# Squares on ScalarE, row-scale chain emitted first, casts and diagonals on GpSimd: one edit in a two-layer mLSTM / sparse-attention kernel

## The chip, the cores and the metric

The kernel runs on 1 core of one Trainium2 chip. The metric is device time in microseconds of one execution; lower is better. A profiled execution has a time of its own and a span, which reaches from its first to its last instruction.

## The reference

A trunk of two layers over 256 tokens of width 1024, in float32. Each layer adds to x a mixer of the RMS-normalised x. Layer 0 is an mLSTM block with four heads of width 512, layer 1 a sparse-attention block with 16 heads. A final RMS norm follows.

```python
def rmsnorm(x, g):
    y = x * lax.rsqrt(jnp.mean(x * x, axis=-1, keepdims=True) + 1e-6)
    return y * g

def mlstm_mixer(h, w_in, conv_w, conv_b, w_q, w_k, w_v, w_if, b_if, ln_w, skip, w_out):
    x_in, z = jnp.split(h @ w_in, 2, axis=-1)                 # 1024 -> 2 x 2048
    conv = sum(x_pad[:, tap:tap + S] * conv_w[tap] for tap in range(4))
    x_conv = jax.nn.silu(conv + conv_b)
    q, k, v = headwise(x_conv, w_q), headwise(x_conv, w_k), headwise(x_in, w_v)   # 4x4 blocks
    gates = jnp.concatenate([q, k, v], -1) @ w_if + b_if
    hh = mlstm_chunkwise(q, k, v, gates ...)
    ...
    return ((hn + skip * x_conv) * jax.nn.silu(z)) @ w_out

x = x + mlstm_mixer(rmsnorm(x, ml_norm), ...)
x = x + nsa_mixer(rmsnorm(x, nsa_norm), ...)
return rmsnorm(x, final_norm)
```

## The kernel before

Every large product is made from three matmuls with operands split in a high and a low part (hi x hi, hi x lo, lo x hi). A weight unit (1 MB) is loaded as two halves (tile wr, SP's queue, L273); ScalarE rounds each half to its high part (wh, L274), and the low part (wl) is the difference, made by VectorE (L280) or, for the units in BY_DMA, by ScalarE and an accumulating DMA from GpSimd's queue (L277, L278). next_unit keeps LOOK = 2 units loaded ahead; ahead(n) writes the loads of the first n units.

The first layer's input comes transposed, as four chunks (xch0). ScalarE makes the high part of x times the gain (hh, L342) and VectorE the low part (hl, L343). The row scale 1/sqrt(mean x^2 + eps) isn't applied to x but to the products: the squares of x (sq1, L354) are summed over chunks (L356, L385), over partitions by a small matmul with ones (L388), get mean and epsilon (L323) and the power -1/2 on GpSimd (L325); two diagonal matrices (dg, L377) and a matmul with ones (L378) spread the result over all partitions, and it is copied to rb1 (L389), with half of it in rb1h (L390). norm1 writes this chain; the first evacuation of the first projection calls it.

The projection of the mLSTM block (project_channels, L411) runs unit by unit into PSUM; evac_x multiplies by rb1 (L438). The loads of cst (masks and block mask), wif (gate weights) and x each wait for rb1 by way of a one-element copy (L441, L445, L448), since they are written behind it in SP's queue. Per head there follow: block-diagonal weights on GpSimd (blockdiag, L398, which needs cst), gate weights on VectorE (L463, L464, which need wif), a convolution of four taps (L476, L480 on ScalarE, L482 on GpSimd, L487 on VectorE), and small projections (L497, L504, L511). In the second layer rstd_of and token_rows are used again for r2.

Instructions are put in each engine's queue when the program is built: a planner walks the written order with a model of the times and gives each engine the earliest written instruction that is ready in the model. So the order in a queue isn't the written one, and on the chip each queue runs strictly in its order.

Of the kernel before, what the change touches and what calls it, by code (L numbers as in the profile page):

```python
# [11 lines left out]
AF = mybir.ActivationFunctionType  # L12
OP = mybir.AluOpType
# [3 lines left out]
P = 128  # L17
S = 256
D = 1024
KT = D // P  # L20
# [37 lines left out]
ZF = 1  # L58
ZT = 3
WARM = 9  # L60
N0 = 2
CA_ = (1, 2, 3)
CB_ = (0,)
CH = 1
SQA = (2, 3)
SQP = (1, 2)
XT = 'zt'
NOT_POOL = (0, 1, 2, 11)
BOTH = (15, 16, 17)
# [133 lines left out]
def trunk(ctx, tc, a, out, dbg=None):  # L203
    nc = tc.nc
# [8 lines left out]
    def tile_of(pl, shape, dt=F32, tag=None, bufs=1, name=None):  # L213
        uid[0] += 1
        n = f"{name or tag}_{uid[0]}"
        return pl.tile(shape, dt, tag=tag or n, bufs=bufs, name=n)

    def T(*x, **k):
        return tile_of(pool[0], *x, **k)

    def TS(*x, **k):
        return tile_of(sb, *x, **k)

    def PS(shape=(P, 512), tag="ps", name="ps"):
        uid[0] += 1
        return pp.tile(list(shape), F32, tag=tag, bufs=PSB[tag], name=f"{name}_{uid[0]}")

    f32 = lambda t: t.bitcast(F32)
    V, A, GP, PE = nc.vector, nc.scalar, nc.gpsimd, nc.tensor
# [9 lines left out]
    xch0 = [T([P, 4, S], tag="zt", bufs=ZT, name="xch0") for _ in range(2)]  # L239
# [9 lines left out]
    pka = T([P, NC_A], name="pka")  # L249
    pkb = TS([P, NC_B], name="pkb")  # L250

    C = lambda n: cst[:, _C[n][0]:_C[n][1]]
    CA = lambda n: pka[:, _A[n][0]:_A[n][1]]
    CB = lambda n: pkb[:, _B[n][0]:_B[n][1]]
    ident = pk0[:, 0:P]
    gain1 = pk0[:, P:]
# [38 lines left out]
    def ahead(n):  # L295
        while len(loaded) < min(n, len(plan)):
            loaded.append(load_unit(*plan[len(loaded)]))
# [11 lines left out]
    first = TS([P, 1], name="first")  # L309
# [9 lines left out]
    def rstd_of(ms, n, name):  # L319

        k = ms.shape[1]
        me = T([P, k], name=name + "me")
        V.tensor_scalar(me, ms, 1.0 / n, 1e-6, op0=OP.mult, op1=OP.add)  # L323
        r = T([P, k], name=name)
        GP.tensor_tensor(r, me, mhalf[:, 0:k], op=OP.pow)  # L325
        return r

    ahead(N0)
    nc.sync.dma_start(pka, a["pka"])

    def transposed(kts, src, gain):

# [7 lines left out]
    def scaled(kts, at, gain):  # L340
        for kt in kts:
            A.activation(hh[:, kt, :], at(kt), AF.Copy, scale=gain[:, kt:kt + 1])  # L342
            V.scalar_tensor_tensor(hl[:, kt, :], at(kt), gain[:, kt:kt + 1], f32(hh[:, kt, :]),  # L343
                                   op0=OP.mult, op1=OP.subtract)

    def new_h():
        return [TS([P, KT, S], F32R, tag="hT", bufs=2) for _ in range(2)]

    hh, hl = new_h()
    sq1 = T([P, 4, S], tag="zt", bufs=ZT, name="sq1")  # L350
    for q in range(4):
        x_ = xch0[q // 2][:, 2 * (q % 2):2 * (q % 2) + 2, :]
        o_ = sq1[:, 2 * min(q, 1):2 * min(q, 1) + 2, :]
        (A.activation(o_, x_, AF.Square) if q in SQA else GP.tensor_tensor(o_, x_, x_, op=OP.mult))  # L354
        if q:
            (GP if q in SQP else V).tensor_tensor(sq1[:, 0:2, :], sq1[:, 0:2, :], o_, op=OP.add)  # L356
    scaled(range(KT), lambda kt: xch0[kt // 4][:, kt % 4, :], gain1)

    def squares(ss, n, tb):
        junk = T([P, 512], tag="sq", bufs=1, name="junk")  # L360
# [2 lines left out]
    def token_scale(ss, name):  # L363

        ms = T([P, 2], name=name + "ms")
        V.tensor_reduce(ms, ss, axis=AX.X, op=OP.add)
        return rstd_of(ms, D, name)
# [4 lines left out]
    def token_rows(r, bank, **place):  # L372

        dg = T([P, 2, P], name="dg", **place)
        ps = PS((P, S), tag=bank)
        for tb in range(2):
            V.tensor_scalar(dg[:, tb, :], ident, r[:, tb:tb + 1], None, op0=OP.mult)  # L377
            PE.matmul(ps[:, tb * P:(tb + 1) * P], onesq, dg[:, tb, :], start=True, stop=True)  # L378
        return ps, dg

    rb1 = T([P, S], name="rb1")
    rb1h = T([P, S], name="rb1h")

    def norm1():
        V.tensor_tensor(sq1[:, 0, :], sq1[:, 0, :], sq1[:, 1, :], op=OP.add)  # L385
        ps = PS((P, 2, 2))
        for tb in range(2):
            PE.matmul(ps[:, tb, :], sq1[:, 0, tb * P:(tb + 1) * P], onesq[:, 0:2], start=True, stop=True)  # L388
        V.tensor_copy(rb1, token_rows(rstd_of(ps[:, :, 0], D, "r1"), "ps")[0])  # L389
        V.tensor_scalar(rb1h, rb1, 0.5, None, op0=OP.mult)  # L390

    spread = lambda r: r[:, None, :].to_broadcast([P, 2, S])

    bm = C("bm")[:, None, :, None].to_broadcast([P, 4, 32, 4])
# [36 lines left out]
    for h in range(NH):  # L431
        xin = T([P, 4, S + 3], tag="xin", bufs=2)
        GP.memset(xin[:, :, 0:3], 0.0)
        for u in range(2):
            def evac_x(ps, x_=xin[:, 2 * u:2 * u + 2, 3:], first=(h, u) == (0, 0)):
                if first:
                    norm1()
                V.tensor_tensor(x_, ps, spread(rb1), op=OP.mult)  # L438
            project_channels(a["wi1"], 2 * h + u, evac_x, ("px", "px", "acc1")[(2 * h + u) % 3])
            if (h, u) == (0, 0):  # L440
                V.tensor_copy(cst[:, 0:1], rb1[:, 0:1])  # L441
                nc.sync.dma_start(cst, a["cst"][:, 0:n_res])
                wifs = [T([P, 16, n // 128, 8], tag="zt", bufs=ZT, name="wif") for n in (1024, 512)]
                for t, o_, n in zip(wifs, (0, 1024), (1024, 512)):
                    V.tensor_copy(t[:, 0, 0, 0:1], rb1[:, 0:1])  # L445
                    nc.sync.dma_start(t.rearrange("p a b c -> p (a b c)"), a["wif"][:, o_:o_ + n])
                for i in range(2):
                    V.tensor_copy(xt[i][:, 0, 0:1], rb1[:, 0:1])  # L448
                    nc.sync.dma_start(xt[i], a["x"][:, i * 512:(i + 1) * 512].rearrange("(t p) c -> p t c", p=P))
# [41 lines left out]
        q = T([P, 4, SG], tag="r4", bufs=8, name="q")  # L491
        gate_weights(q[:, :, S:SG], wqk, wifs[0], 2)
        for c2 in range(2):
            ps = PS((P, 2, S))
# [6 lines left out]
        for tb in range(2):  # L501
            ps = PS((P, 3, PG), tag="pt")
# [6 lines left out]
        ps = PS()  # L509
# [9 lines left out]
        scs.append(sc)  # L519

    ident_r = TS([P, P], F32R, name="ident_r")
    V.tensor_copy(ident_r, ident)
    maskt_r = T([P, 2, P], F32R, name="maskt_r")
    V.tensor_copy(maskt_r, C("maskt")[:, None, :].to_broadcast([P, 2, P]))
    causal = C("mask2")

    vsps = []
# [52 lines left out]
    ps = PS((P, 2, 64))  # L580
# [10 lines left out]
    for h in range(NH):  # L591
# [25 lines left out]
        r = sm("r")  # L617
# [28 lines left out]
    for h in range(NH):  # L646
# [8 lines left out]
        for c2 in range(2):  # L655
            ps = PS((P, 2, S))
# [4 lines left out]
            for c in range(2):  # L661
                k = 2 * c2 + c
                V.scalar_tensor_tensor(y[:, k, :], ps[:, c, :], lnw[:, 4 * h + k:4 * h + k + 1], y[:, k, :],
                                       op0=OP.mult, op1=OP.add)
# [79 lines left out]
    transposed(range(4, 8), x_cols, gain2)  # L744
    r2 = token_scale(ss2, "r2")
    ps, dg = token_rows(r2, "acc0", tag="p0", bufs=PB)
    rb = T([P, S], name="rb")
    V.tensor_copy(rb, ps)
# [395 lines left out]
```

## Time and profile before

| | us |
|---|---|
| three runs | 380.86, 381.38, 384.1 |
| median | 381.38 |
| profiled execution, time | 378.87 |
| profiled execution, span | 377.1 |
| mean granted TensorE clock | 0.984 |

The profiled execution lies 2.5 us under the median of the runs. In the profile, PE is TensorE's matmuls, DVE is VectorE, ACT is ScalarE, POOL is GpSimd, SP issues most loads. "Idle" stands in brackets at the end of a row of the timeline, with what ended it; a row that merges several instructions says so by x and a number.

### The profile page before, as it was taken

Reading aid. Unit: us, or ns where it says so; the run is one execution under the profiler, and the core shown is the slowest. Engines: PE = TensorE matmul, PEld = TensorE weight load, DVE = VectorE, ACT = ScalarE, POOL = GpSimd, SP = SyncE. Lnnn points to the kernel's source line nnn. Section 1 sums busy time; section 2 is a strip of 40 time slices with the busy share of each in tenths; the row PEclk is TensorE's granted clock in tenths of the full one; section 3 lists DMA queues with packets and bytes.
Section 4 is the critical chain, followed back from the end, with each engine's and each line's share of the span. In section 5 each row is a group of like instructions: output and inputs, shape, how many; then the busy total and the mean of one; then the engine's idle time right before and its main releaser. Section 6 shows DMA issues by size and latency. Waiting matters only on the chain.

```text
span 377.1 us, 6621 instructions
## 1 busy us (share of the span) xinstructions
PE 350.6 (93%) x2399; PEld 313.8 (83%) x2399; DVE 255.7 (68%) x535; ACT 241.5 (64%) x438; POOL 134.7 (36%) x165
## 2 busy tenths in 40 slices
PE   6998799979999979999999799999879999999991
PEld 6998799869998968988887699999869996777771
DVE  5976999756476548983243736687979789684515
ACT  6674669738468649765653744372579789996304
POOL 5226377433301124610100303283430283857003
PEclk9999899999999999999999999999989999999997
DMA  7889758765646978999998897546577865020003
GB/s 260 280 269 315 209 129 217 188 152 125 167 157 159 197 210 217 228 233 296 239 262 239 266 343 216 173 104 155 154 195 209 246 237 158 2 56 2 2 0 112
DMA packets 21633, 69.57 MB, mean 185 GB/s; under 512 B 2528, under 2 KB 2912, under 8 KB 21600
## 3 DMA queue, kind: packets, MB, share of 16 engines
q1 hardware_dynamic: 15472, 48.71, 38.7%
q0 software_dynamic: 4752, 16.83, 24.6%
q10 hardware_dynamic: 1376, 3.61, 2.9%
q8 instruction: 19, 0.31, 0.3%
q14 instruction: 14, 0.11, 0.1%
HBM read 50.87 MB, written 1.05 MB: 138 GB/s over the span
## 4 chain that ended last, share of the span: by engine, by line
PE 39%; DMA 23%; DVE 18%; issue 8%; ACT 8%; POOL 1%; SPq 1%; ACTq 0%; POOLq 0%; DVEq 0%
PE ps L411 17%; DMA wl<-wr 7%; DMA wr<-in_wo_dram 6%; DVE xc L487 6%; PE ps L694 6%; DVE wl L280 4%; DMA wr<-in_wi2z_dram 3%; DMA wr<-in_wi2k_dram 2%; ACT wh L274 2%; PE ps L984 2%; PE ps L909 2%; PE ps L897 2%; DMA cst<-in_cst_dram 2%; DMA xch<-in_xt_dram 1%; ACT wl L277 1%
## 5 line engine op out<-in xcount | busy, mean ns | idle before, releaser
L411 PE MATMUL ps<-hT,wh 128*128 128x256 f32 x832 | 139.5, 293 | 2.4 <-DVE hT L343 1.3
L274 ACT ACTIVATE wh<-wr 128x1024 fp32r<-128x1024 f32 (+2 forms) x90 | 89.5, 1000 | 58.1 <-PE ps L411 21.5
L411 PEld LDWEIGHTS ps<-hT,wh 128*128 128x128 f32 x832 | 121.8, 198 | 4.6 <-DVE hT L343 1.9
L280 DVE TENSOR_TENSOR wl<-wr,wh 128x1024 fp32r<-128x1024 f32 (+2 forms) x57 | 70.9, 1244 | 36.0 <-ACT wh L274 33.2
L411 PE MATMUL ps<-hT,wl 128*128 128x256 f32 x416 | 87.7, 287 | 0.0
L411 PEld LDWEIGHTS ps<-hT,wl 128*128 128x128 f32 x416 | 66.4, 193 | 1.0 <-issue 0.6
L278 POOL DMA_DIRECT2D wl<-wr x33 | 28.7, 877 | 107.9 <-ACT wl L277 103.5
L277 ACT ACTIVATE wl<-wr 128x1024 fp32r<-128x1024 f32 (+1 forms) x33 | 33.8, 1025 | 13.4 <-PE ps L694 6.6
L694 PE MATMUL ps<-wh,r 128*128 128x512 f32 x128 | 41.4, 398 | 0.0
L487 DVE SCALAR_TENSOR_TENSOR xc<-xin,pka,xc 128x256 f32<-128x256 f32 x44 | 30.8, 754 | 0.1
L694 PEld LDWEIGHTS ps<-wh,r 128*128 128x128 f32 x128 | 24.0, 188 | 5.5
L694 PE MATMUL ps<-wl,r 128*128 128x512 f32 x64 | 25.3, 395 | 0.0
L694 PE MATMUL ps<-wh,y 128*128 128x512 f32 x64 | 21.8, 406 | 0.0
L803 POOL TENSOR_TENSOR swap<-swap,trig 128x512 f32<-128x512 f32 x6 | 10.2, 1697 | 18.9 <-DMA swap<-qu 7.3
L775 PE MATMUL ps<-wl,hT 128*128 128x280 f32 (+1 forms) x48 | 15.8, 330 | 1.2 <-DMA wl<-wr 1.2
L846 PE MATMUL ps<-ka,qt 128*128 128x256 f32 (+1 forms) x32 | 12.0, 380 | 3.8 <-DVE nm L852 3.7
L774 PE MATMUL ps<-wh,hT 128*128 128x280 f32 (+1 forms) x48 | 15.5, 329 | 0.0
L776 PE MATMUL ps<-wh,hT 128*128 128x280 f32 (+1 forms) x48 | 15.2, 325 | 0.0
L694 PEld LDWEIGHTS ps<-wh,y 128*128 128x128 f32 x64 | 11.8, 188 | 3.1 <-issue 0.8
L694 PEld LDWEIGHTS ps<-wl,r 128*128 128x128 f32 x64 | 12.0, 188 | 2.8 <-DMA wl<-wr 0.2
L641 POOL TENSOR_TENSOR xc<-xc,pka 128x1024 f32<-128x1024 f32 x4 | 9.8, 2455 | 12.2 <-PE ps L512 12.2
L504 PE MATMUL ps<-m,xin 128*128 128x136 f32 x64 | 9.7, 299 | 3.6 <-DVE m L464 3.5
(473 smaller groups left out, 676.0 us busy)
## 6 DMA issues: line engine op xcount, KB each, us to landing
wr<-in_wi_dram SPq DMA_DIRECT2D x34, 512.0 KB
wl<-wr POOLq DMA_DIRECT2D x31, 512.0 KB, 5.9
wr<-in_wo_dram SPq DMA_DIRECT2D x24, 512.0 KB
wr<-in_wi2k_dram SPq DMA_DIRECT2D x12, 512.0 KB
wr<-in_wi2z_dram SPq DMA_DIRECT2D x8, 512.0 KB
wr<-in_wi2v_dram SPq DMA_DIRECT2D x8, 280.0 KB
cw<-in_cw_dram ACTq DMA_DIRECT2D x4, 512.0 KB
xch<-in_xt_dram SPq DMA_DIRECT2D x4, 256.0 KB
```

Of the source, the lines that this page charges most:

```text
L274: A.activation(hi[:, k, :], raw[:, k, :], AF.Copy)
L277: A.activation(lo[:, k, :], raw[:, k, :], AF.Copy, scale=-1.0)
L278: GP.dma_start(out=lo[:, k, :].rearrange("p k n -> p (k n)"), in_=raw[:, k, :].rearrange("p k n -> p (k n)"), accum_op=OP.add)
L280: V.tensor_tensor(lo[:, k, :], raw[:, k, :], f32(hi[:, k, :]), op=OP.subtract)
L411: PE.matmul(ps[:, c, :], w, (hl if i == 1 else hh)[:, k, :], start=(k, c, i) == (0, 0, 0), stop=(k, i) == (KT - 1, 2), skip_group_check=True)
L487: V.scalar_tensor_tensor(xc[:, c, :], xin[:, c, tap:tap + S], tap_w(tap, c), xc[:, c, :], op0=OP.mult, op1=OP.add)
L694: PE.matmul(acc, l, r[:, k % 2, cols], start=first and i == 0, stop=last and i == 2)
L774: PE.matmul(o_, lh, hi[:, k % 2, :], start=kt == 0, stop=False)
L775: PE.matmul(o_, lh, lo[:, k % 2, :], start=False, stop=False)
L776: PE.matmul(o_, ll, hi[:, k % 2, :], start=False, stop=kt == KT - 1)
L803: (GP, V)[RE[1]].tensor_tensor(sw, sw, turn(1), op=OP.mult)
L846: PE.matmul(o_, lq, ka[:, g, :, 0:w_], start=True, stop=False)
```

## The change

The squares of x all run on ScalarE and all their additions on VectorE. The scaling of x (hh, hl) is written ahead of the squares. norm1 is called right after its definition and not in the first evacuation. Only the first unit's load is written before that; the second unit's and pka follow norm1. In rstd_of the mean-and-epsilon step runs on ScalarE, in token_rows the diagonals on GpSimd, both in the second layer too. rb1h is made on ScalarE. The casts to ident_r and maskt_r run on GpSimd.

```diff
@@ -58,12 +58,12 @@
 ZF = 1
 ZT = 3
 WARM = 9
-N0 = 2
+N0 = 1
 CA_ = (1, 2, 3)
 CB_ = (0,)
 CH = 1
 SQA = (2, 3)
-SQP = (1, 2)
+SQP = ()
 XT = 'zt'
 NOT_POOL = (0, 1, 2, 11)
 BOTH = (15, 16, 17)
@@ -320,13 +320,12 @@
 
         k = ms.shape[1]
         me = T([P, k], name=name + "me")
-        V.tensor_scalar(me, ms, 1.0 / n, 1e-6, op0=OP.mult, op1=OP.add)
+        A.activation(me, ms, AF.Copy, scale=1.0 / n, bias=1e-6)
         r = T([P, k], name=name)
         GP.tensor_tensor(r, me, mhalf[:, 0:k], op=OP.pow)
         return r
 
     ahead(N0)
-    nc.sync.dma_start(pka, a["pka"])
 
     def transposed(kts, src, gain):
 
@@ -347,14 +346,14 @@
         return [TS([P, KT, S], F32R, tag="hT", bufs=2) for _ in range(2)]
 
     hh, hl = new_h()
+    scaled(range(KT), lambda kt: xch0[kt // 4][:, kt % 4, :], gain1)
     sq1 = T([P, 4, S], tag="zt", bufs=ZT, name="sq1")
     for q in range(4):
         x_ = xch0[q // 2][:, 2 * (q % 2):2 * (q % 2) + 2, :]
         o_ = sq1[:, 2 * min(q, 1):2 * min(q, 1) + 2, :]
-        (A.activation(o_, x_, AF.Square) if q in SQA else GP.tensor_tensor(o_, x_, x_, op=OP.mult))
+        A.activation(o_, x_, AF.Square)
         if q:
             (GP if q in SQP else V).tensor_tensor(sq1[:, 0:2, :], sq1[:, 0:2, :], o_, op=OP.add)
-    scaled(range(KT), lambda kt: xch0[kt // 4][:, kt % 4, :], gain1)
 
     def squares(ss, n, tb):
         junk = T([P, 512], tag="sq", bufs=1, name="junk")
@@ -374,7 +373,7 @@
         dg = T([P, 2, P], name="dg", **place)
         ps = PS((P, S), tag=bank)
         for tb in range(2):
-            V.tensor_scalar(dg[:, tb, :], ident, r[:, tb:tb + 1], None, op0=OP.mult)
+            GP.tensor_scalar(dg[:, tb, :], ident, r[:, tb:tb + 1], None, op0=OP.mult)
             PE.matmul(ps[:, tb * P:(tb + 1) * P], onesq, dg[:, tb, :], start=True, stop=True)
         return ps, dg
 
@@ -387,8 +386,11 @@
         for tb in range(2):
             PE.matmul(ps[:, tb, :], sq1[:, 0, tb * P:(tb + 1) * P], onesq[:, 0:2], start=True, stop=True)
         V.tensor_copy(rb1, token_rows(rstd_of(ps[:, :, 0], D, "r1"), "ps")[0])
-        V.tensor_scalar(rb1h, rb1, 0.5, None, op0=OP.mult)
-
+        A.activation(rb1h, rb1, AF.Copy, scale=0.5)
+
+    norm1()
+    ahead(2)
+    nc.sync.dma_start(pka, a["pka"])
     spread = lambda r: r[:, None, :].to_broadcast([P, 2, S])
 
     bm = C("bm")[:, None, :, None].to_broadcast([P, 4, 32, 4])
@@ -432,9 +434,7 @@
         xin = T([P, 4, S + 3], tag="xin", bufs=2)
         GP.memset(xin[:, :, 0:3], 0.0)
         for u in range(2):
-            def evac_x(ps, x_=xin[:, 2 * u:2 * u + 2, 3:], first=(h, u) == (0, 0)):
-                if first:
-                    norm1()
+            def evac_x(ps, x_=xin[:, 2 * u:2 * u + 2, 3:]):
                 V.tensor_tensor(x_, ps, spread(rb1), op=OP.mult)
             project_channels(a["wi1"], 2 * h + u, evac_x, ("px", "px", "acc1")[(2 * h + u) % 3])
             if (h, u) == (0, 0):
@@ -519,9 +519,9 @@
         scs.append(sc)
 
     ident_r = TS([P, P], F32R, name="ident_r")
-    V.tensor_copy(ident_r, ident)
+    GP.tensor_copy(ident_r, ident)
     maskt_r = T([P, 2, P], F32R, name="maskt_r")
-    V.tensor_copy(maskt_r, C("maskt")[:, None, :].to_broadcast([P, 2, P]))
+    GP.tensor_copy(maskt_r, C("maskt")[:, None, :].to_broadcast([P, 2, P]))
     causal = C("mask2")
 
     vsps = []
```

## Rows read from the trace of the kernel before

**Rows 1.** The page, part 1: busy time, share, instructions.
```profile
PE 350.6 (93%) x2399; PEld 313.8 (83%) x2399; DVE 255.7 (68%) x535; ACT 241.5 (64%) x438; POOL 134.7 (36%) x165
```
**Rows 2.** TensorE's waits, whole span: us in total, times, longest.
```profile
PE ps L504 <- DVE m L464: 3.5, 1, 3.5
PE ps L497 <- DVE gsc L516: 2.4, 1, 2.4
...
PE ps L378 <- ACT hT L342: 1.6, 1, 1.6
PE ps L411 <- DVE hT L343: 1.3, 2, 0.9
```
**Rows 3.** Windows of TensorE alone: us, busy (records), granted clock, DMA share, GB/s.
```profile
36.50:40.00 3.50, 0.03 (x1) 1.00 0.63 252
40.00:44.30 4.30, 4.30 (x24) 0.63 0.89 187
44.30:48.60 4.30, 4.30 (x38) 0.97 0.61 198
```
**Rows 4.** The chain that ended last, first 60 us: start, us, what.
```profile
25.97 6.04 DMA cst<-in_cst_dram
```
**Rows 5.** Timeline of VectorE, 0 to 34 us: start, us, instruction, [idle before].
```profile
4.70 0.99 DVE L522 CAST ident_r<-pk 128x128 fp32r<-128x128 f32 x1 [4.70 <-DMA pk<-in_pk_dram]
...
6.41 1.52 DVE L280 TENSOR_TENSOR wl<-wr,wh 128x512 fp32r<-128x512 f32 x1
...
9.67 0.68 DVE L280 TENSOR_TENSOR wl<-wr,wh 128x512 fp32r<-128x512 f32 x1
...
14.80 0.43 DVE L385 TENSOR_TENSOR sq<-sq 128x256 f32<-128x256 f32 x1
...
20.17 0.48 DVE L377 TENSOR_SCALAR dg<-pk,r 128x128 f32<-128x128 f32 x2 [0.61 <-POOL r L325]
...
24.53 0.42 DVE L389 COPY rb<-ps 128x256 f32<-128x256 f32 x1 [1.37 <-PE ps L378]
...
32.04 0.29 DVE L524 CAST maskt_r<-cst 128x256 fp32r<-128x256 f32 x1 [2.26 <-DMA cst<-in_cst_dram]
```
**Rows 6.** Line 487, 28 to 60 us: duration ns min/median/max, first and last start.
```profile
L487 DVE SCALAR_TENSOR_TENSOR xc<-xin,pka,xc x20: 471/478/2595, 32.2 to 55.9; 128x256 f32<-128x256 f32 x20
```
**Rows 7.** Line 343, 0 to 20 us, the same columns.
```profile
L343 DVE SCALAR_TENSOR_TENSOR hT<-xch,pk,hT x8: 471/472/1505, 5.6 to 13.1; 128x256 fp32r<-128x256 f32 x8
```
**Rows 8.** Timeline of GpSimd, 0 to 34 us.
```profile
9.81 1.69 POOL L356 TENSOR_TENSOR sq<-sq 128x512 f32<-128x512 f32 x1 [0.74 <-ACT sq L354]
18.51 1.63 POOL L325 TENSOR_TENSOR r<-r1me,mhalf 128x2 f32<-128x2 f32 x1 [7.01 <-DVE r1me L323]
...
32.15 1.09 POOL L398 TENSOR_TENSOR m<-AT,cst 128x512 f32<-128x512 f32 x1 [2.95 <-DMA cst<-in_cst_dram]
```
**Rows 9.** Timeline of TensorE, 0 to 34 us.
```profile
17.21 0.50 PE L388 MATMUL ps<-onesq,sq 128*128 128x2 f32 x4
...
23.88 0.61 PE L378 MATMUL ps<-dg,onesq 128*128 128x128 f32 x4
```
**Rows 10.** Timeline of ScalarE, 0 to 34 us.
```profile
9.10 0.63 ACT L354 ACTIVATE sq<-xch 128x512 f32<-128x512 f32 x1
...
12.06 1.99 ACT L274 ACTIVATE wh<-wr 128x1024 fp32r<-128x1024 f32 x2
```
**Rows 11.** Window of all engines: PE, PEld, DVE, ACT, POOL busy, clock, DMA.
```profile
4.70:14.70 10.00, 7.72 (x37) 6.84 (x36) 10.00 (x14) 8.70 (x16) 5.40 (x4) 1.00 0.94 345
```
**Rows 12.** GpSimd's groups by shape: busy us, mean ns | idle before.
```profile
L865 POOL TENSOR_SCALAR p__492_2867<-p__492_2867,sums,gt 128x128 f32<-128x128 f32 x2 | 0.9, 445 | 0.0
```
**Rows 13.** Timeline of ScalarE, 24 to 75 us.
```profile
64.76 0.27 ACT L515 ACTIVATE sc<-ps 128x128 f32<-128x128 f32 x1
```
**Rows 14.** Timeline of VectorE, 203 to 228 us.
```profile
210.35 1.48 DVE L323 TENSOR_SCALAR r2me<-r2ms 128x2 f32<-128x2 f32 x1
```
**Rows 15.** Timeline of TensorE, 203 to 228 us.
```profile
213.16 0.68 PE L378 MATMUL ps<-dg,onesq 128*128 128x128 f32 x4 [1.64 <-ACT hT L342]
```

## The prediction

> **What bounds the kernel now.** I read the shares of the engines first. TensorE is busy for 93% of the span and no other engine for more than 68% [rows 1], so a change to the other engines can save only what TensorE stands idle or runs slowly because of them. The table of TensorE's waits says where that is [rows 2]. In the part that the change touches first, the reader is to see 1.3 us for the low part of the scaled input (hl, L343), and 3.5 us at L504, the value projection of the first head, for the gate weights that VectorE reduces (L464). Then 2.4 us come at L497, again behind VectorE, and 1.6 us at L378 in the second layer.
>
> The wait at L504 costs more than its length. By the windows, TensorE is empty from 36.5 to 40.0; from 40.0 to 44.3 its granted clock is 0.63 of full and 24 matmul records fit in, and in the next 4.3 us, at 0.97, there are 38 [rows 3]. 14 records fewer at 4.3/38 = 0.113 us are 1.6 us, so the price of this wait is 3.5 + 1.6 = 5.1 us.
>
> The chain of waits tells why VectorE is late there. The load of cst is issued when rb1, the row scale, exists, and takes 6.04 us from 25.97 [rows 4]. On VectorE the cast of the mask (maskt_r, L524) stands in the queue ahead of the convolution, and VectorE idles 2.26 us before it until cst has landed [rows 5]. The convolution itself (L487) takes 0.48 us at the median, but up to 2.6 us [rows 6]; the long ones stand beside GpSimd's block-diagonal products (L398), which begin at 32.15 [rows 8].
>
> **The change part by part.**
>
> *Squares, casts and the start.* The two GpSimd squares and two GpSimd additions go; the second addition alone held GpSimd for 1.69 us from 9.81 [rows 8]. Beside such work, VectorE's subtraction for wl (L280, 128x512) took 1.52 us at 6.41, and 0.68 us at 9.67 when GpSimd was idle [rows 5]; the hl steps take 0.472 us at the median and at most 1.505 [rows 7]. So squares on GpSimd stretched VectorE's work. First the row, then the rule: the 1.52 against 0.68 is what the Trainium skill (SBUF — State Buffer, Who interferes with whom) would have, where VectorE's instructions with two SBUF inputs and GpSimd's reads exclude each other; the trace agrees, and by the same rule the casts and diagonals that now go to GpSimd can block VectorE again, some 0.5 us at a time.
>
> The ident_r cast leaves VectorE too; it took 0.99 us from 4.70, ahead of the first hl step [rows 5]. VectorE gets two more additions of squares, at about the price of a subtraction of the same size, 0.68 us at most [rows 5], or 1.4 us together. They come after hl in the written order, so the first matmuls don't wait for them. What I count is TensorE's wait for hl, 1.3 us [rows 2]: -1.3 us. Its bounds are 0 (the x transfers end it instead) and -2.2 (those 1.3 and the 0.99 us of the cast; small gaps between the hl steps close as well).
>
> ScalarE pays two more squares at 0.63 us [rows 10], 1.26 us. In the ten microseconds from 4.70 it is busy 8.70 us [rows 11], so they nearly fill it. Queued behind them are the wh conversions of the second weight unit, at 12.06 before [rows 10]. TensorE was still on the first unit and the squares' sums at 17.21 [rows 9], so about 3 us of matmuls hide a delay of 1.3 us; without that cover it would cost the 1.3.
>
> *The chain to the row scale.* Before, the last sum of squares was ready at 14.80 + 0.43 = 15.23 [rows 5], but TensorE took it at 17.21; the diagonals were ready at 20.65 [rows 5] and TensorE took them at 23.88 [rows 9]. So 2.0 + 3.2 us of the chain are place in TensorE's queue, not work. The queue order is planned when the program is built, from the written order and a model of the times; norm1 now stands ahead of all matmuls and of the second unit's loads, so both steps should be taken closer to when they are ready. The work of the chain hardly falls. The mean-plus-epsilon step on ScalarE costs some 0.27 us by the nearest row, a PSUM read of 128x128 [rows 13]. The power stays at 1.63 us [rows 8]. The two diagonals on GpSimd cost 2 x 0.45 us by the tensor-scalar row of that shape [rows 12], where both took 0.48 us on VectorE [rows 5]: +0.4. The Trainium skill (GPSIMD Engine Reference, 4.1 Engine selection) would leave elementwise work on VectorE; the rows agree on the price, and by it alone this chain gets longer. With about half of the 5.2 us of queue place gone, the sums 1 us earlier and 0.6 us more of work, rb1 comes near 22 instead of 24.95 [rows 5]. rb1h on ScalarE is used only by the gate path much later; I cost it at nothing, and what hides it is the whole first projection. If ScalarE reached it early, it would hold the weight conversions behind it for the wait.
>
> The three loads behind rb1 (cst, wif, x) move up in SP's queue with it and past some wi loads; these run several units ahead of TensorE, which waits for no weight load before 40 [rows 2]. pka stays behind the second unit's loads.
>
> *The wait at L504.* Three things pull its last input forward: rb1 by 3 us, the mask's cast out of VectorE's way by 2.26 us [rows 5], and some convolution steps that now run before the block-diagonal products and not beside them. Together this is more than the wait. But TensorE's place for L504 is planned by the same model and will be planned earlier too; what the plan misjudged (4 to 5 us of slow steps on VectorE) is only partly gone. The ends are 0 (the wait moves with the work) and -5.1; I take -3.1, nearer to the lower end, since the idle before maskt_r goes for certain. Next late is VectorE itself, at L497: the same head start takes -1.0 from that wait (0 to -2.4 [rows 2]).
>
> *Second layer.* rstd_of and token_rows serve r2 as well. TensorE stands at L378 there until 213.16, idle for 1.64 us [rows 15], and nothing covers the step: the two diagonals on GpSimd add 0.4 us. The mean step took 1.48 us on VectorE [rows 14] and may become 0.27 on ScalarE, or wait there behind a 128x1024 conversion, 1.0 us [rows 10]. I take +0.5, bounds -0.8 and +1.5.
>
> The sum is -1.3 - 3.1 - 1.0 + 0.5 = -4.9 us. The profiled execution took 378.87 us (span 377.1), so it would become 374.0. It was faster than the median of the three runs, 381.38, by 2.5; against the median the forecast is 376.5.
>
> **The rivals.** (1) The stall only moves. TensorE's queue puts L504 early again and VectorE is as late against the plan as before. For it: the plan doesn't know the slow steps of L487. Against it: the mask's cast is gone. Only the start's 1.3 less the second layer's 0.5 remain: 380.6 us.
>
> (2) The chain doesn't get earlier. The written order is not the order run: the ident_r cast is written after the first stage and ran first [rows 5]. Then TensorE takes both steps of the chain as late as now, and the gain is the start (-1.3), the idle before the mask's cast as far as TensorE sees it (-2.26 of the 3.5 at L504) and +0.5: 378.3 us.
>
> (3) Slower: TensorE's queue places the small steps too early. It works in order, so L388 or L378, planned ahead of the matmuls that hid the chain, stops all of them until the chain has caught up. The cover is now 2.0 us at L388 and 3.2 us at L378. Without it L388 waits some 2 us for the squares on the full ScalarE, L378 waits for mean, power and diagonals, 0.27 + 1.63 + 0.9 = 2.8 us, and one spell of the lower clock adds 1.6: 6.4 us. If L504 comes early as well (the 5.1 us stay), the time is 381.4 - 1.3 + 6.4 + 0.5 = 387.0 us. It decides from 4.9 us of waits and lost clock together, where the gain is eaten up. For it: the chain now runs over four engines. Against it: at both steps the plan was late before, never early.
>
> **How the numbers follow.** Chances: forecast 0.50, the stall moves 0.16, the chain stays 0.17, too early 0.17. One per cent, about 3.8 us, is what a measurement of this kernel can tell from no change, so faster means under 377.6. The forecast's own range is 370.5 to 380, and some 0.38 of its 0.50 lie under 377.6; the chain that stays gives 0.08 there and the stall that moves 0.03. That makes faster 0.49. Of the too-early case 0.13 lies above 385.2, and a plan that shifts waits of later stages, of the size of those at L504 and L497, adds 0.04: slower 0.17, same 0.34. The bounds of the terms add to -9.9 at the lower end and +1.5 at the upper; with the too-early case partly inside, the range is 370 to 385.
>
> **What would show it.** Right: no GpSimd square in the first 12 us and hl steps near 0.47 us; L388 and L378 taken within 1 us of being ready; rb1 near 22; cst issued before 24; no VectorE idle ahead of the convolution; a wait at L504 under 2 us and a granted clock near 1 from 36 to 48; the diagonals in the second layer at 0.45 us each on GpSimd. Wrong: a wait at L388 or L378 in the first 25 us, a new low of the clock, or TensorE's waits after 84 us larger than those shown, which would mean that the new plan costs more later than the start gains.

## The result and the profile after

The changed kernel takes 383.25 us at the median of 20 runs, the kernel before 379.57 in the same session. The ratio is 1.013, with a 95% interval of 1.010 to 1.016: slower, where 376.5 and a gain were forecast. The three runs of before that the forecast started from had a median of 381.38; from 379.57 its gain of 4.9 us would lead to 374.7. The profiled execution has a span of 380.8 us (before: 377.1). Executions over 1.5% above the fastest of their kernel count in the medians here but not in the ratios, and no time is read from the profiles of e4, e6, e9 and e12, which fell on such executions.

TensorE works as long as before (350.9 us against 350.6); of the 3.7 us, 3.4 are idle time of TensorE. First the page, part 1, of the changed kernel, against [rows 1]:

```profile
PE 350.9 (92%) x2399; PEld 313.2 (82%) x2399; DVE 249.1 (65%) x528; ACT 242.2 (64%) x443; POOL 124.3 (33%) x167
```

VectorE and GpSimd are less busy and TensorE is not quicker for it. Next the views that answer to [rows 5, 8 to 10], all of the first 50 us after the change. (Old lines 343, 385, 388, 378, 389, 377 and 398 are now 342, 384, 387, 377, 388, 376 and 400; from L438 on the numbers agree.) VectorE:

```profile
15.91 0.42 DVE L384 TENSOR_TENSOR sq<-sq 128x256 f32<-128x256 f32 x1
...
25.23 0.42 DVE L388 COPY rb<-ps 128x256 f32<-128x256 f32 x1 [0.58 <-PE ps L377]
...
34.13 1.59 DVE L463 TENSOR_TENSOR wtmp<-wif,pka 128x128 f32<-128x128 f32 x2 [5.12 <-DMA wif<-in_wif_dram]
...
42.80 0.48 DVE L487 SCALAR_TENSOR_TENSOR xc<-xin,pka,xc 128x256 f32<-128x256 f32 x1
```

ScalarE, GpSimd and TensorE, the same stretch:

```profile
19.68 0.15 ACT L323 ACTIVATE r1me<-ps 128x2 f32<-128x2 f32 x1
```

```profile
19.98 1.62 POOL L325 TENSOR_TENSOR r<-r1me,mhalf 128x2 f32<-128x2 f32 x1 [14.94 <-ACT r1me L323]
21.70 1.20 POOL L376 TENSOR_SCALAR dg<-pk,r 128x128 f32<-128x128 f32 x2
...
36.58 0.45 POOL L524 CAST maskt_r<-cst 128x256 fp32r<-128x256 f32 x1
37.00 2.71 POOL L482 TENSOR_TENSOR xc<-xc,x 128x512 f32<-128x512 f32 x2
```

```profile
19.12 0.50 PE L387 MATMUL ps<-onesq,sq 128*128 128x2 f32 x4
...
24.10 0.39 PE L377 MATMUL ps<-dg,onesq 128*128 128x128 f32 x2
```

The start is as forecast: no square on GpSimd. The chain is not. The last sum of squares is ready at 16.33 and TensorE takes it at 19.12, 2.8 us later; the first rb1 stands at 25.65 (before: 24.95), so cst, wif and x are asked for after 26. VectorE then idles 5.12 us for wif, and the convolution begins at 42.80 and not at 32.2 [rows 6]: its GpSimd step (L482) is queued behind five block-diagonal products and the cast of the mask, and VectorE's own queue has gate weights (L463, L464) ahead of it, with which VectorE is busy nearly all the time from 34.13 to 42.8.

TensorE's waits, the view of [rows 2], first up to 200 us, then from there to the end:

```profile
PE ps L413 <- DVE wl L280: 2.6, 1, 2.6
PE ps L694 <- DMA wl<-wr: 1.9, 2, 1.4
PE ps L413 <- ACT wh L274: 1.5, 1, 1.5
PE ps L497 <- ACT xc L489: 1.4, 1, 1.4
PE ps L504 <- DVE m L464: 1.1, 1, 1.1
...
```

```profile
PE ps L774 <- ACT hT L341: 4.1, 1, 4.1
PE ps L1007 <- DVE kcb L1001: 2.4, 1, 2.4
PE ps L775 <- DMA wl<-wr: 1.6, 1, 1.6
PE ps L413 <- DMA wl<-wr: 1.2, 1, 1.2
PE ps L413 <- ACT wh L274: 0.8, 1, 0.8
PE ps L913 <- ACT pt L906: 0.7, 1, 0.7
PE ps L909 <- DVE pt L901: 0.6, 1, 0.6
PE ps L905 <- ACT pt L899: 0.3, 1, 0.3
```

The kernel before, the same view from 200 us on:

```profile
PE ps L846 <- DVE nm L852: 3.7, 2, 2.6
PE ps L378 <- ACT hT L342: 1.6, 1, 1.6
PE ps L775 <- DMA wl<-wr: 1.2, 1, 1.2
```

Up to 200 us all rows of this view add to 12.1 us before and 10.3 after; from there on to 6.5 before and 11.7 after. So the loss lies in the second layer, which the change touches in two small steps. The times of the first layer's output projection (L694) and of the last residual addition (L716) say the same; the columns are durations in ns (min/median/max), then first and last start. Before:

```profile
L694 PE MATMUL ps<-wh,r x128: 388/395/481, 156.9 to 203.2; 128*128 128x512 f32 x128
L716 DVE TENSOR_TENSOR x<-ps,x x8: 681/691/693, 178.9 to 369.5; 128x512 f32<-128x512 f32 x8
```

After:

```profile
L694 PE MATMUL ps<-wh,r x128: 388/395/482, 151.5 to 201.0; 128*128 128x512 f32 x128
L716 DVE TENSOR_TENSOR x<-ps,x x8: 681/688/692, 176.2 to 373.2; 128x512 f32<-128x512 f32 x8
```

The first layer's output projection begins 5.4 us earlier and ends 2.2 us earlier: it grew from 46.3 to 49.5 us, with 2.7 us of waits that it did not have before (1.9 for weight halves by DMA, 0.8 for VectorE's x). Windows over it (columns as in [rows 11]) show the DMA engines as full as before, 0.96 and 0.95:

```profile
156.00:204.00 48.00, 48.00 (x221) 39.02 (x221) 23.80 (x32) 30.42 (x37) 9.54 (x9) 1.00 0.96 256
```

```profile
156.00:204.00 48.00, 45.17 (x195) 35.47 (x194) 17.16 (x20) 25.72 (x31) 6.01 (x7) 1.00 0.95 251
```

The second layer, from 203.2 to 369.5 before, takes 166.3 us; from 201.0 to 373.2 after, 172.2. So -5.4 + 3.2 + 5.9 = +3.7 us, the difference of the spans. Of the 5.9, 5.2 are the longer waits.

### The profile page after: what moved, and what is told of

Same layout as the page of the kernel before. It is cut to its first block, busy times and chain, and to the rows that moved or that the text cites. A ratio compares the mean times of both kernels' runs of the same rounds, so it can differ in the third digit from the quotient of the medians.

```text
span 380.8 us, 6627 instructions
## 1 busy us (share of the span) xinstructions
PE 350.9 (92%) x2399; PEld 313.2 (82%) x2399; DVE 249.1 (65%) x528; ACT 242.2 (64%) x443; POOL 124.3 (33%) x167
## 4 chain that ended last, share of the span: by engine, by line
PE 56%; DMA 17%; DVE 13%; ACT 5%; issue 4%; SPq 1%; POOL 1%; ACTq 0%; POOLq 0%; DVEq 0%
PE ps L413 27%; DMA wl<-wr 8%; PE ps L694 7%; DVE xc L487 3%; PE ps L497 2%; DVE wl L280 2%; PE ps L615 2%; PE ps L984 2%; PE ps L909 2%; PE ps L511 2%; PE ps L897 2%; DMA wr<-in_wo_dram 2%; DMA wif<-in_wif_dram 2%; ACT wh L274 2%; DVE wtmp L463 2%
## 5 line engine op out<-in xcount | busy, mean ns | idle before, releaser
L413 PE MATMUL ps<-hT,wh 128*128 128x256 f32 x832 | 138.0, 290 | 2.4 <-ACT wh L274 2.4
L413 PEld LDWEIGHTS ps<-hT,wh 128*128 128x128 f32 x832 | 119.7, 195 | 4.8 <-ACT wh L274 2.9
L280 DVE TENSOR_TENSOR wl<-wr,wh 128x1024 fp32r<-128x1024 f32 (+2 forms) x57 | 67.6, 1188 | 45.0 <-ACT wh L274 44.8
L413 PE MATMUL ps<-hT,wl 128*128 128x256 f32 x416 | 87.7, 287 | 3.8 <-DVE wl L280 2.6
L413 PEld LDWEIGHTS ps<-hT,wl 128*128 128x128 f32 x416 | 66.2, 192 | 4.9 <-DVE wl L280 2.8
L278 POOL DMA_DIRECT2D wl<-wr x33 | 28.8, 882 | 107.4 <-ACT wl L277 92.3
L694 PE MATMUL ps<-wh,r 128*128 128x512 f32 x128 | 41.1, 398 | 0.8 <-DVE x L716 0.8
L277 ACT ACTIVATE wl<-wr 128x1024 fp32r<-128x1024 f32 (+1 forms) x33 | 33.9, 1027 | 12.5 <-DMA wr<-in_wo_dram 5.0
L694 PEld LDWEIGHTS ps<-wh,r 128*128 128x128 f32 x128 | 24.0, 188 | 6.7 <-issue 1.2
L694 PE MATMUL ps<-wl,r 128*128 128x512 f32 x64 | 25.6, 399 | 2.0 <-DMA wl<-wr 1.9
L487 DVE SCALAR_TENSOR_TENSOR xc<-xin,pka,xc 128x256 f32<-128x256 f32 x44 | 25.9, 647 | 0.2 <-ACT xc L476 0.2
L694 PE MATMUL ps<-wh,y 128*128 128x512 f32 x64 | 21.3, 403 | 0.0
L774 PE MATMUL ps<-wh,hT 128*128 128x280 f32 (+1 forms) x48 | 15.9, 341 | 4.1 <-ACT hT L341 4.1
L775 PE MATMUL ps<-wl,hT 128*128 128x280 f32 (+1 forms) x48 | 16.2, 339 | 1.6 <-DMA wl<-wr 1.6
L694 PEld LDWEIGHTS ps<-wl,r 128*128 128x128 f32 x64 | 12.0, 188 | 5.8 <-issue 1.8
L803 POOL TENSOR_TENSOR swap<-swap,trig 128x512 f32<-128x512 f32 x6 | 7.8, 1300 | 23.0 <-DMA swap<-qu 11.8
L694 PEld LDWEIGHTS ps<-wh,y 128*128 128x128 f32 x64 | 11.9, 189 | 2.8 <-issue 0.4
L774 PEld LDWEIGHTS ps<-wh,hT 128*128 128x128 f32 x48 | 9.2, 195 | 5.2 <-ACT hT L341 4.5
L694 PE MATMUL ps<-wl,y 128*128 128x512 f32 x32 | 12.8, 401 | 0.0
```

The costliest lines, as they stand in the source:

```text
L277: A.activation(lo[:, k, :], raw[:, k, :], AF.Copy, scale=-1.0)
L278: GP.dma_start(out=lo[:, k, :].rearrange("p k n -> p (k n)"), in_=raw[:, k, :].rearrange("p k n -> p (k n)"), accum_op=OP.add)
L280: V.tensor_tensor(lo[:, k, :], raw[:, k, :], f32(hi[:, k, :]), op=OP.subtract)
L413: PE.matmul(ps[:, c, :], w, (hl if i == 1 else hh)[:, k, :], start=(k, c, i) == (0, 0, 0), stop=(k, i) == (KT - 1, 2), skip_group_check=True)
L487: V.scalar_tensor_tensor(xc[:, c, :], xin[:, c, tap:tap + S], tap_w(tap, c), xc[:, c, :], op0=OP.mult, op1=OP.add)
L694: PE.matmul(acc, l, r[:, k % 2, cols], start=first and i == 0, stop=last and i == 2)
```

## The experiments

The theory after this reading was that the planner gives the later queues another order whenever anything ahead changes, and that the order it now found is worse. The rival was the direct one: the second layer's row scale, r2, has a longer chain on its new engines. All kernels were timed against the kernel before in five rounds, in three sessions (e1 to e4, e5 to e8, e9 to e12); each ratio is to the kernel before of its own session. Where two queues are compared below, that is by lines and tiles of their instructions, in the order in which the traces have them.

**e1, e2, e3: the second layer's steps.** e1 is the changed kernel with both steps of r2 back on VectorE, e3 the one with the mean step alone back, e2 the kernel before with the two r2 diagonals on GpSimd.

```diff
-        A.activation(me, ms, AF.Copy, scale=1.0 / n, bias=1e-6)
+        A.activation(me, ...) if name == "r1" else V.tensor_scalar(me, ...)
...
-            GP.tensor_scalar(dg[:, tb, :], ident, r[:, tb:tb + 1], None, op0=OP.mult)
+            (GP if bank == "ps" else V).tensor_scalar(dg[:, tb, :], ident, ...)
```

> The changed kernel with the second layer's mean step and diagonals back on VectorE; everything of the first layer as changed. Theory A (the second layer's row-scale chain, 8.43 us after and 3.84 us before from its sums to rb, gives the gain of the first layer away): the lead of some 5 us at the start of the first output projection lives on in part, ratio to before 0.985 to 0.995, and the chain takes under 5 us again. Theory B (a lead is used up by the weight loads of the output projection and by a new plan of the later stages, whoever runs the chain): ratio 1.00 to 1.015, with a lead at 150 us that is gone by 285 us.

> The kernel before with only the second layer's two diagonals on GpSimd. The first layer's queues are those of before. Theory A: two steps of 0.6 us in place of 0.24 us, on TensorE's wait in the second layer, so 0.5 to 1.5 us: ratio 1.002 to 1.004, unless the new order of the later queues costs more. Theory B (the new order of the later queues is what costs): the same kind of waits as after at the compressed values (L1007) and in the last third, ratio 1.007 to 1.015.

> The changed kernel with only the second layer's mean step back on VectorE; the order of TensorE's queue is nearly that of after. There the step stood 2.45 us on ScalarE behind a weight conversion that waited for its load. Theory A: the chain to rb shortens by some 2 us and so does the time: ratio to before 1.007 to 1.009. Theory B: the gain is taken by the next wait, ratio 1.011 to 1.015.

Measured: e1 386.97 us, 1.0203 (1.016 to 1.0246); e2 381.91 us, 1.0036 (0.9997 to 1.0075); e3 384.83 us, 1.0158 (1.0131 to 1.0185). Giving r2 its old engine makes nothing better: e1 lies above both of its expected ranges, e3 just above the range of theory B. In e1 and e3 the second layer still takes 172.3 and 172.4 us, and e3, whose queues in the second layer are nearly those of the changed kernel, still waits 4.0 us at L774. So the loss does not need r2's new engines. In e2, where two small instructions alone have moved, TensorE's wait for kcb appears too (2.3 us), and the second layer takes 168.8; but its ratio lies in the range of theory A and under that of B.

The traces say where the new order comes from. In e2 the first layer's queues are those of before, and TensorE's queue in the second layer is nearly that of the changed kernel (some 50 of 1,150 instructions stand elsewhere): moving the two r2 diagonals is enough for it. In e1 only the first layer differs from before, and the second layer gets a third order, with the worst time of all.

**e4: the written order alone**, all engines as before.

> The kernel before with only the written order changed: norm1, the scaling and the loads written as in the changed kernel, every step on the engine of before. The queues differ little from before. My forecast said that writing the chain first takes 2.6 us of queue place out of it; then rb1 comes near 22.5 us and the ratio is 0.99 to 0.995. The rival (the chain does not get earlier, since the planner takes a step when its inputs are ready in its model): rb1 at 24.5 to 25.5 us, ratio 0.997 to 1.003.

Measured: 381.08 us, 1.0035 (0.9996 to 1.0074): no difference that can be measured. Its diff is the part of the change that moves lines and loads, with no engine changed. In the trace the queues of e4 are those of the kernel before on every engine, SP's included (but for one pair on ScalarE, whose starts lie within 0.1 us of each other): the planner puts these steps where it put them, wherever they are written. So here it is the moves to other engines that make a new plan, and not any edit ahead, as the theory had it.

**e5, e6, e7, e8: the old order of the queues.** Here each engine's queue is held in the order that it has in the kernel before, from a mark in the program on, by edges between neighbours in the queue; they carry no wait. Instructions whose engine differs from before are left free.

```diff
+    mark = int(nc.cur_bb.bb.instructions[-1].name[2:])
...
+    traced = {i.name: i for i in nc.cur_bb.bb.instructions}
+    for q in QUEUES.values():
+        for i, j in zip(q, q[1:]):
+            tc.add_manual_dep(traced[f"I-{mark + j}"], f"I-{mark + i}", DependencyInfo(NoSync, DATA))
```

e5 is the changed kernel with this for the second layer, e6 is e1 with the same, e7 the changed kernel with the mark where the casts are written, behind the convolution stage. e8 has every move to another engine, the written order of before, and all queues held.

> The changed kernel, with every engine's queue of the second layer put into the order of the kernel before (edges that only order a queue, no waits); the mean step and the two diagonals on their new engines are left to the planner. Theory B (the new order of the second layer's queues is what costs): from the last product of the first layer to the end, before took 166 us and after 172; with the old order 166 to 168 us, and the ratio to before falls from 1.013 to 0.995 to 1.003. Theory A (the engines of the second layer's row-scale chain cost it) and theory C (the weight loads in the first layer's output projection use the lead up, whatever the second layer does): the second layer stays near 172 us, ratio 1.010 to 1.016.

> The kernel of the first experiment (only the first layer changed, 1.020) with the second layer's queues in the order of before. Theory B: ratio 0.993 to 1.003, the second layer at 166 us. Rival: stays at 1.012 or above.

> The changed kernel with the queue orders of before from the casts on, that is for the gates, the stabilised products, the output projection and the second layer; only the convolution stage and what is ahead of it are as the new plan has them. Theory B with a lead from the first stage: ratio 0.990 to 1.000, TensorE at the output projection 2 to 5 us ahead of before, and that lead half kept to the end. Theory C: no better than the run with only the second layer's queues fixed.

> The kernel before with every step on the engine of the changed kernel, the written order of before, and all queues in the order of before; only the moved steps themselves are placed anew. My forecast's terms of engines alone: the start (-1.3), the mask's cast out of VectorE's way (-2.3 at most) and the second layer (+0.5): ratio 0.992 to 0.998. If the moves cost by themselves (diagonals and casts on GpSimd beside VectorE, the mean step behind ScalarE's conversions): 1.003 to 1.010.

Measured: e5 378.19 us, 0.9988 (0.9961 to 1.0016); e6 380.54 us, 0.9995 (0.9953 to 1.0036), against 1.0203 for the same kernel as e1; e7 376.47 us, 0.9929 (0.9894 to 0.9964); e8 376.51 us, 0.9921 (0.9883 to 0.9959). The same instructions on the same engines as in the changed kernel lose all of the 1.3% once the second layer runs in the old order. The traces confirm the edits: in e5 the first layer's queues are those of the changed kernel, and TensorE's queue in e8 is that of before from end to end. TensorE's waits of e5 from 200 us on (this profiled execution, 376.04 us, lies 2.2 under the median):

```profile
PE ps L846 <- DVE nm L852: 3.3, 2, 2.6
PE ps L377 <- POOL dg L376: 2.0, 1, 2.0
```

The waits at L774, L1007 and for the weight halves are gone. What is left is 5.3 us against 6.5 before and 11.7 after, and the second layer takes 165.2 us:

```profile
L694 PE MATMUL ps<-wh,r x128: 388/395/482, 152.0 to 201.4; 128*128 128x512 f32 x128
L716 DVE TENSOR_TENSOR x<-ps,x x8: 680/687/693, 176.4 to 366.6; 128x512 f32<-128x512 f32 x8
```

**e9, e10: the order by itself.** e9 puts the new order into the old kernel: all engines and the first layer as before, and the second layer's queues as in the changed kernel. e10 is e5 with TensorE's queue alone held. The edit is that of e5, with other lists.

> The kernel before with all its engines and its first layer, but the queues of the second layer put in the order that they have in the changed kernel, by order edges without a wait. Theory (the new order of the later queues costs some 6 us): slower than before, 1.010 to 1.018, and the span from the last product of the first layer to the last of the second near 172 us against 166.3. Rival (the order edges themselves, or something else in the pinned kernels, make them quick, and the order is harmless): 0.990 to 1.003. If the new order is bad only because the changed first layer feeds it at other times: 1.000 to 1.008.

> The changed kernel with TensorE's queue alone put back in the order of before in the second layer; the queues of ScalarE, VectorE, GpSimd and SP stay as the new plan has them. If the order on TensorE carries the loss: as with all queues put back, 0.996 to 1.004. If the order of the engines that feed it carries it (weight halves, copies of the value products): 1.008 to 1.020, or slower still, since TensorE then waits for work that the others have queued later.

Measured: e9 382.91 us, 1.007 (1.0032 to 1.0109). The new order makes the kernel before slower, and edges are not what makes a kernel quick. But it is less than the 1.010 that the theory asked for; it lies where the case stood in which the first layer's timing counts as well. In its trace the second layer's order is the changed kernel's but for a few instructions around r2. With e2, which has nearly this order and 1.0036, the new order by itself costs 0.4 to 0.7%.

e10: 380.72 us, 1.0048 (1.0014 to 1.0081). Neither expectation was met, and the edit did not do what it was meant to: with TensorE's queue held, the planner gave the other engines nearly the old order too. In the traces of e10 and e5 TensorE's second-layer queue is the same, and on each other engine seven instructions or fewer stand elsewhere, all between 203 and 215 us. There the planner has kept one thing of the new order: on ScalarE a weight conversion (L277), which waits 1.68 us for its load, stands ahead of r2's mean step; in e5 it stands behind. So e10 against e5 does not tell TensorE's order from that of the engines that feed it; it gives the price of r2's place. The wait for kcb is gone, but TensorE waits 4.0 us for the diagonals where e5 waits 2.0:

```profile
211.82 1.39 PE L377 MATMUL ps<-dg,onesq 128*128 128x128 f32 x4 [4.00 <-POOL dg L376]
```

From 212 to 216 us the granted clock is then 0.50 in e10 and 1.00 in e5. The product L975 begins at 226.3 in e10 and at 222.9 in e5, and the last addition at 370.2 and 366.6: the difference of that place stays to the end. In the ratios, which come from different sessions, it is 0.6%; the other 0.8% of the 1.4% between the changed kernel and e5 go with the order that was put back.

**e11, e12: the moves without the written order.** e11 is e8 without the held queues, so planned anew. e12 is e8 with r2 left on VectorE.

> The kernel before with every move to another engine and none of the changes in the written order; the queues are planned anew. With the queues held in the order of before the same moves gave 0.9921. Theory (a new plan costs what the moves gain): 1.003 to 1.018. Rival (the loss comes from the changed written order, not from planning anew): 0.988 to 0.996.

> The kernel before with the squares on ScalarE, the casts, the mean step and the diagonals of the first layer moved, and those of the second layer left on VectorE; all queues in the order of before. If the moved steps of the second layer cost what their chain got longer (4.6 us at most, 0.5 us by the prediction): 0.980 to 0.991. If they cost nothing with the old order: 0.991 to 0.994.

Measured: e11 383.7 us, 1.013 (1.0087 to 1.0172), against 0.9921 in e8. The two differ in nothing but the order of the queues, by 2.1% (in two sessions, but the intervals are far apart); in the second layer TensorE's queue in e11 is the changed kernel's, instruction for instruction. e12: 377.07 us, 0.9928 (0.9894 to 0.9963), as e8: in the old order, where r2's steps run is worth nothing that can be measured. TensorE's waits of e11 from 200 us on begin like those of the changed kernel, in the same two places:

```profile
PE ps L774 <- ACT hT L342: 3.6, 1, 3.6
PE ps L1007 <- DVE kcb L1001: 2.4, 1, 2.4
```

**How an order makes a wait.** The wait for kcb is one of the two large ones, and the trace shows all of it. VectorE in the changed kernel around 250 us, then GpSimd and TensorE there:

```profile
248.09 3.32 DVE L816 TENSOR_TENSOR kb<-rot,ka 64x1024 fp32r<-64x1024 f32 x1
251.44 2.53 DVE L1004 COPY h1r<-h1T 128x512 f32<-128x512 f32 x1
254.00 2.20 DVE L816 TENSOR_TENSOR kb<-rot,ka 64x1024 fp32r<-64x1024 f32 x1
256.23 0.69 DVE L797 TENSOR_TENSOR qu<-ps,rb 128x512 f32<-128x512 f32 x1
256.84 0.45 DVE L1001 COPY kcb<-ps 64x64 f32<-64x64 f32 x2
```

```profile
247.74 5.95 POOL L816 TENSOR_TENSOR kb<-rot,ka 64x1024 fp32r<-64x1024 f32 x2
```

```profile
257.43 1.08 PE L1007 MATMUL ps<-pkb,h1r 128*128 128x64 f32 x8 [2.36 <-DVE kcb L1001]
```

Before, the copy L1004 stood later in VectorE's queue, clear of GpSimd's two products:

```profile
260.31 0.43 DVE L1004 COPY h1r<-h1T 128x512 f32<-128x512 f32 x1
```

It takes 2.53 us beside them and 0.43 without, a step of L816 up to 3.32 where the shorter one took 1.22 before. The new order places the copy beside GpSimd and kcb behind it. With the short durations (1.22, 0.43, 1.22, 0.69 and 0.45 from 248.09) kcb would be ready at 252.1, and TensorE came to L1007 at 255.1: in a plan without the stretch that is no wait. This is an estimate from the durations; no run had the copy at another place alone. Before, TensorE took L1007 at 265.9 and waited for nothing.

The other large wait shows in the changed kernel's ScalarE at 208 us:

```profile
208.51 1.06 ACT L277 ACTIVATE wl<-wr 128x1024 fp32r<-128x1024 f32 x1 [1.52 <-DMA wr<-in_wi2k_dram]
...
209.47 0.19 ACT L323 ACTIVATE r2me<-r2ms 128x2 f32<-128x2 f32 x1
209.56 1.04 ACT L274 ACTIVATE wh<-wr 128x1024 fp32r<-128x1024 f32 x1
```

The conversion of a weight half that has not landed is queued ahead of r2's mean step, another conversion and ScalarE's own DMA issues (to 211.17) behind it, and hT, which TensorE's L774 needs, comes only at 211.22. In e5, where TensorE comes to this place as early, it waits 2.0 us. TensorE is empty from 207.6 to 211.7, and then its granted clock is 0.53 of full for 3.3 us, near the lower of its two levels (1.2 of 2.4 GHz):

```profile
207.60:211.70 4.10, 0.06 (x1) 1.00 0.98 373
211.70:215.00 3.30, 3.26 (x10) 0.53 0.99 286
```

## Why the prediction was wrong

Two steps failed. The one that cost the time is the sum, "-1.3 - 3.1 - 1.0 + 0.5 = -4.9 us". It was made for the queues of before; a new plan of all that follows got a chance of 0.04 and no term. What the runs showed in its place: the second layer, for which the sum has +0.5, lost 5.9 us, and its old order gives back all of the 1.3% (e5); between two orders of the same instructions lie 2.1% (1.013 in e11 against 0.9921 in e8).

The other is "norm1 now stands ahead of all matmuls and of the second unit's loads, so both steps should be taken closer to when they are ready", from which "rb1 comes near 22". Writing the chain first changes no queue (e4). Rival (2), "The written order is not the order run", holds: TensorE took the sums at 19.12 and the diagonals at 24.10, where it had been 17.21 and 23.88 [rows 9]. The sums were ready 2.8 us and the second diagonal (22.90) 1.2 us before that, and of "within 1 us" neither held. Point by point:

- *The start, -1.3.* Right as an event: the wait for hl is gone, the steps take 0.48 us each at the most. TensorE now waits 1.52 us there for wh on ScalarE, where 1.0 us stood before; so the waits fell by 0.8 us. TensorE is further ahead than that: by 19 us 89 of its records have run since 5 us, against 71 before, which at 0.12 us each is 2.2 us, the term's lower bound: matmuls (L411, wl) that took 0.41 us one by one around 13 us take 0.28 now. That is not the same in every build: in e8, with TensorE's queue of before, the sums are taken 0.5 us earlier (16.72).
- *The chain.* Rival (2), as above. But rb1's time also decides less than I took it to: in e7 rb1 stands at 27.34, 2.4 us later than before, and the kernel is 0.7% faster.
- *L504, -3.1, and L497, -1.0.* The wait at L504 fell from 3.5 to 1.1 us and the clock there is 1.00 where it was 0.63 [rows 3]. The forecast rested on an earlier convolution, and that came 10.6 us later; it was the gate weights that VectorE now makes ahead of it. So this term came near its size by luck. And the stall moved on, as rival (1) has it: VectorE's convolution delays a weight half (2.6 us at L413) and L497 (1.4), and from 54 to 60 the clock is 0.57, in this window of TensorE:

```profile
54.00:60.00 6.00, 4.60 (x17) 0.57 0.47 156
```

- *Second layer, +0.5, bounds to +1.5.* The chain from the sums to the copy of r2 grew from 3.84 to 8.43 us, 4.6, beyond its bound. Most of that is place in queues: 1.6 us on TensorE, which takes L377 at 214.36 when the diagonals are ready at 212.77, 1.0 until the mean step on ScalarE is done, behind the conversion, and 0.7 before the power, behind GpSimd's own DMA issue (L278). The longer steps on GpSimd are 1.0 (power 1.04 us against 0.72, diagonals 1.20 against 0.48). With the old order the moves of r2 cost nothing that can be measured (e5 and e6, e8 and e12). The whole layer, which the prediction left alone but for this term, lost 5.9 us.
- *A gain ahead of a stage that is bound by loads.* The sum let each microsecond of the first layer reach the end. Of the 5.4 us ahead at 151 us, 3.2 went in the output projection, at a DMA share of 0.95. That e8 keeps only 2.2 us of lead at its start and 0.4 at its end speaks for the same cause; no run tried other loads there.
- *"TensorE's waits after 84 us larger than those shown, which would mean that the new plan costs more later than the start gains"* is what the prediction named as its refutation, and what came: 14.4 us against 9.0.
- *Readings.* The lower bounds of the four terms add to -10.5 and not to -9.9. And the 0.68 us of VectorE's subtraction at 9.67 is no row "when GpSimd was idle": GpSimd's addition began at 9.81 [rows 8], 0.14 us after it, and took 1.69 us. The squares and additions did stretch VectorE's steps all the same: the hl steps, up to 1.505 us before, take 0.48 at the most without them.

With all moves in the old order the forecast of a gain comes true: e8 gives 0.9921, 3.0 us of the 4.9 of the sum. But this is in part luck, as its waits do not go by the sum's terms. They add to 15.6 us against 18.6 before. Of the waits that the sum names, L497 fell by 1.1 as forecast; the 1.3 for hl went and 1.4 more came for wh; the stall at L504 (3.5) fell to 0.7 at the first head, and one of 3.6 stands at the second. What fell besides, L615 by 2.3 and L775 by 1.2, the sum did not hold. (The profiled execution of e8, 378.32 us, lies 1.8 over its median and shows less of the gain in the span.) The wait at the second head:

```profile
PE ps L504 <- DVE xin L438: 3.6, 1, 3.6
```

What stays open: e9 and e2 put 0.4 to 0.7% on the new order by itself, and the changed kernel lost 1.4% by it; how the rest divides between the first layer's earlier handing over and the free instructions was not told apart. Nor was each of the smaller new waits (weight halves, pt) followed to its cause. The quickest versions are e7 and e8, 0.7 and 0.8% under the kernel before and about 2% under the changed one.

## What to carry to other kernels

Where a planner fills the queues, a step that moves to another engine can replan everything behind it (in e1 the second layer, from moves in the first), while moving lines in the program may change nothing (e4): ask what the new order does to stages that the edit does not touch, compare the queues of both builds before the time is forecast, and give that a price (here 2% between two orders of the same instructions). To learn what an edit itself is worth, hold the other queues in their old order, all of them, and look in the trace whether the order is the one that was meant: with one queue held, the planner changed the others too (e10). And a lead that is won ahead of a stage whose loads fill the DMA engines has to be followed through it before it is counted.

## What the runs showed of the hardware beyond what was expected

Small GpSimd instructions took more than twice as long in one run as in another, and what differs in the trace is what VectorE does beside them. The power of two columns took 0.71 us in e8 with VectorE idle and 1.62 in the changed kernel beside VectorE's subtraction for wl. The two diagonals, forecast at 0.9 us, took 1.20 there with VectorE idle, and in e8 2.95 beside two such subtractions. VectorE is not the only cause: the power of r2 in the changed kernel took 1.04 us with VectorE idle, while GpSimd's own DMA issue was running. GpSimd in e8:

```profile
17.58 0.71 POOL L325 TENSOR_TENSOR r<-r1me,mhalf 128x2 f32<-128x2 f32 x1 [12.59 <-ACT r1me L323]
18.39 2.95 POOL L377 TENSOR_SCALAR dg<-pk,r 128x128 f32<-128x128 f32 x2
```

and VectorE there:

```profile
18.41 2.46 DVE L280 TENSOR_TENSOR wl<-wr,wh 128x1024 fp32r<-128x1024 f32 x2 [1.50 <-ACT wh L274]
```

The prediction priced this sharing against VectorE alone; here GpSimd's instruction is the one that waits. The Trainium skill (SBUF — State Buffer, Who interferes with whom) calls the shared pair of ports an exclusive lock between the two engines, and both directions agree with that: 2.95 against 1.20 us here, and VectorE's copy L1004, which took 2.53 us and ended at 253.97, just after GpSimd's second product (253.69).
